# A two-layer encoder on one core: the mixers' tokens column by column, narrow windows for mixer B, and its probabilities turned by 12 short copies

## The chip, the cores and the metric

One core of one Trainium2 chip runs the whole program in one launch. The metric is the device time of a run in microseconds (us), lower is better. TensorE is called PE (its weight loads PEld), VectorE DVE, ScalarE ACT, GpSimd POOL; SP issues the transfers (DMA).

## The reference

256 tokens of width 2048 pass through two layers, all in fp32. Each layer has a mixer sub-layer and a feed-forward network; both are modulated by shifts, scales and gates that a vector `c` gives through a 2048 x 12288 matrix (adaLN).

```python
for l in range(DEPTH):
    mod = c_act @ ada_w[l] + ada_b[l]
    h = rmsnorm(x, norm_mix[l]) * (1.0 + sc_a) + sh_a
    qa, ka, va, qb, kb, vb, ga, gb = split_cols(h @ w_in[l])
    ya = window_attention(qa, ka, va, sink_a[l]) @ w_proj_a[l]
    yb = neighbourhood_attention(qb, kb, vb, rel_bias_b[l]) @ w_proj_b[l]
    merged = jax.nn.sigmoid(ga) * ya + jax.nn.sigmoid(gb) * yb
    x = x + gt_a * (merged @ w_out[l])
    h = rmsnorm(x, norm_ffn[l]) * (1.0 + sc_m) + sh_m
    g, v = jnp.split(depthwise_conv(h @ w_up[l], conv_w[l], conv_b[l]), 2, axis=-1)
    x = x + gt_m * ((jax.nn.silu(g) * v) @ w_down[l])
```

Mixer A (8 query heads, 2 key heads of 128) sees tokens at most 128 apart, with rotary positions and a sink. Mixer B (8 heads) sees the tokens as a grid of 4 rows by 64 columns; a token attends to all 4 rows and 16 neighbouring columns, with a learned bias by relative position. The feed-forward network is 5632 wide and has a convolution of width 3 over the tokens, in their plain order.

## The kernel before

**Data.** Features lie on the 128 partitions, 16 chunks of them, and the 256 tokens along the free axis. The weights come in one long stream `ws`, in the order in which they are used, as units of 16 blocks of 128 x 128 (1 MB). Each unit is loaded by SP into one of four raw buffers (line 315, a tile `w{layer}_{unit}`) and split in two halves `hl{layer}_{unit}_{half}` into a high and a low part: ACT copies (L326), DVE subtracts (L327). The high and low parts are rounded to fp32r, a format that PE takes faster than fp32. Each block then costs three matmuls of 256 columns (L343 to L345), or, where tokens and not features become the rows (the q, k, v columns), of 512 columns (L406 to L408). Between the units SP loads the adaLN matrix in blocks of 1 MB (`aw{layer}_{n}`, L232) into the same raw buffers; DVE multiplies and adds up each of them (L233) to 128 numbers. SP's transfers start in the order in which they are written, and they use eight completion semaphores in rotation.

**Start.** The first norm makes the chunks of h one by one (`normed`): ht (L497), its high part (ACT, L500) and its low part (L501). A chunk needs the adaLN numbers of its own blocks, so the start alternates aw blocks, units w_0, w_1, ... and the chunks of h. The columns of q, k, v are walked in two passes over k (`pi` 0 and 1) in nine groups of 512 columns (`g` 0 to 8). In layer 0 the tables of mask and of cosine and sine are loaded by `small` at the second pass's first group (L789).

**Attention.** Heads are Python generators that run beside the weight stream. `attend` (L646) does one head: scores `sc` for two halves of 128 queries (L651), in fp32 in layer 0 and as three fp32r matmuls in layer 1; one DVE instruction per half adds mask or bias and takes the maximum (L654), writing into the tile `p`; exp (L662) and scaling (L670) on ACT; then p is turned so that keys lie on partitions. In layer 0 PE turns it by four transposes (L681). In layer 1 DVE turns 32 x 32 blocks within each 32 partitions (L304) into free slots of the pack (the tile of q, k, v of four heads), and POOL moves the blocks between partitions by 16 copies of 32 x 128 back into p (L298). The result is split into `pT` (ACT L418, DVE L421), and six matmuls with v give `po` (L689). For mixer B, `head_b` (L876) loads the head's 256 KB bias by one transfer into one of two buffers `p` (L880), and the same tile then holds scores and probabilities until they are split.

**Merge.** The projections of the mixers are gated and added: `gated` (L434) makes m, L1014 adds ya, `split` (L423, L424) gives `merged`, the input of `w_out`. In layer 1 the gate of A is made by `bare_gate` from a tile z through tanh into `ya`.

**Order.** The program is written with generators; a scheduler then sets the order on each engine from estimated costs and priorities, so instructions move by more than the diff shows.

## Time and profile before

| | us |
|---|---|
| median of 3 runs | 2655.18 |
| lowest, highest | 2653.85, 2655.35 |
| the profiled execution | 2661.45 |
| its span in the trace | 2659.6 |

The profiled execution is 6.3 us longer than the median, and 1.85 us of it lie outside the span. Times inside the trace are counted from the span's start. The share of each engine and the groups of instructions are shown in the prediction; in the views quoted there "x16" is a count, "276/276/276" are the shortest, middle and longest duration in ns, and `[0.58 <-ACT h L500]` is idle time before an instruction and what ended it. Buffer numbers are left out of names there: `aw` is any block of the adaLN matrix, `hl` any half of a unit. Matmul durations overlap, so the distance between two starts is the cost, and not the duration. Stages used below, in us from the start: the start up to 100; mixer B's heads of layer 0 at 341 to 445; the merge of layer 0 about 490 to 595; mixer B's heads of layer 1 at 1622 to 1740.

### The profile page before, as it was taken

The numbers are of one execution on the slowest core, as the hardware profiler recorded it, in microseconds if no ns is written. First come the engines' busy times: TensorE is split into PE (matmuls) and PEld (weight loads), VectorE is DVE, ScalarE is ACT, GpSimd is POOL, SyncE is SP. The second block draws the span as 40 slices with busy tenths as digits, with TensorE's granted clock in tenths as the row PEclk, the third lists the DMA queues.
The fourth block names the chain that finished last, engine by engine and source line by source line (L and its number), as shares of the span: only waits on it lengthen the run. The fifth ranks groups of instructions, "written<-read, shape, count | busy, mean of one in ns | idle before, by whom it ended". The sixth has DMA issues, their size and how long they took to land.

```text
span 2659.6 us, 51014 instructions
## 1 busy us (share of the span) xinstructions
PE 2643.3 (99%) x21164; PEld 2557.9 (96%) x21164; DVE 2121.0 (80%) x2979; ACT 1408.9 (53%) x2280; POOL 228.2 (9%) x345
## 2 busy tenths in 40 slices
PE   9999999999999999999999999999999999999999
PEld 7888899999999999999998889999999999999999
DVE  8898998997987888788886778868888866655664
ACT  5445865456643555355554666654565445544553
POOL 0001100000000000000002558520000000000000
PEclk9999999999999999999999999999999999999999
DMA  9987779885777777877766666666747765555554
GB/s 371 349 329 292 267 294 356 316 339 184 295 272 289 284 287 285 306 296 285 283 221 253 249 234 232 253 258 257 283 178 287 297 252 191 192 196 194 196 191 143
DMA packets 102042, 700.42 MB, mean 263 GB/s; under 512 B 12721, under 2 KB 15025, under 8 KB 17969
## 3 DMA queue, kind: packets, MB, share of 16 engines
q1 hardware_dynamic: 101810, 697.17, 70.8%
q8 instruction: 165, 2.70, 0.4%
q14 instruction: 67, 0.55, 0.1%
HBM read 695.03 MB, written 2.10 MB: 262 GB/s over the span
## 4 chain that ended last, share of the span: by engine, by line
PE 86%; DMA 5%; DVE 5%; issue 2%; ACT 1%; POOL 0%; SPq 0%; DVEq 0%; ACTq 0%
PE ps L343 24%; PE ps L345 24%; PE ps L344 24%; DMA aw<-in_aw 4%; PE ps_t L408 4%; PE ps_t L407 4%; PE ps_t L406 4%; DVE hl L327 2%; DVE aw L233 1%; PE sc L651 1%; ACT hl L326 1%; PE po L689 1%; DMA w<-in_ws 1%; DVE u L1049 0%; POOL qrs L472 0%
## 5 line engine op out<-in xcount | busy, mean ns | idle before, releaser
L327 DVE TENSOR_TENSOR hl<-w,hl 128x1024 fp32r<-128x1024 f32 x928 | 1129.8, 1224 | 298.0 <-ACT hl L326 294.7
L326 ACT CAST hl<-w 128x1024 fp32r<-128x1024 f32 x928 | 969.8, 1049 | 719.7 <-PE ps L345 501.4
L343 PE MATMUL ps<-h,hl 128*128 128x256 f32 x3328 | 922.4, 277 | 1.3 <-DVE ya L970 0.6
L344 PE MATMUL ps<-h,hl 128*128 128x256 f32 x3328 | 919.6, 276 | 0.0
L345 PE MATMUL ps<-h,hl 128*128 128x256 f32 x3328 | 919.6, 277 | 0.0
L343 PEld LDWEIGHTS ps<-h,hl 128*128 128x128 f32 x3328 | 624.7, 188 | 2.4 <-DVE ya L970 0.8
L344 PEld LDWEIGHTS ps<-h,hl 128*128 128x128 f32 x3328 | 625.3, 188 | 0.4 <-DVE h L501 0.2
L345 PEld LDWEIGHTS ps<-h,hl 128*128 128x128 f32 x3328 | 624.4, 188 | 0.0
L233 DVE CUSTOM_DVE_ANT_0 aw<-aw,cact,ab 128x2048 f32<-128x2048 f32 x189 | 443.8, 2349 | 92.5 <-DMA aw<-in_aw 91.7
L406 PE MATMUL ps_t<-hl,h 128*128 128x512 f32 x576 | 223.0, 392 | 2.7 <-ACT h L500 2.0
L407 PE MATMUL ps_t<-hl,h 128*128 128x512 f32 x576 | 225.0, 391 | 0.3
L408 PE MATMUL ps_t<-hl,h 128*128 128x512 f32 x576 | 224.3, 390 | 0.0
L1049 DVE SCALAR_TENSOR_TENSOR u<-ps,cw,u 128x255 f32<-128x255 f32 x304 | 146.0, 480 | 62.0 <-ACT u L1047 58.1
L1047 ACT ACTIVATE u<-ps,cw 128x256 f32<-128x256 f32 x152 | 85.7, 564 | 155.4 <-PE ps L345 155.2
L343 PE MATMUL ps<-act_o,hl 128*128 128x256 f32 x512 | 142.0, 278 | 2.7 <-DVE u L1049 2.6
L345 PE MATMUL ps<-act_o,hl 128*128 128x256 f32 x512 | 142.1, 278 | 1.3 <-DVE hl L327 1.3
L344 PE MATMUL ps<-act_o,hl 128*128 128x256 f32 x512 | 142.0, 277 | 0.0
L345 PE MATMUL ps<-merged,hl 128*128 128x256 f32 x512 | 141.5, 277 | 0.0
L344 PE MATMUL ps<-merged,hl 128*128 128x256 f32 x512 | 141.5, 276 | 0.0
L343 PE MATMUL ps<-merged,hl 128*128 128x256 f32 x512 | 141.5, 277 | 0.0
L406 PEld LDWEIGHTS ps_t<-hl,h 128*128 128x128 f32 x576 | 107.9, 188 | 26.1 <-ACT h L500 3.0
L407 PEld LDWEIGHTS ps_t<-hl,h 128*128 128x128 f32 x576 | 108.1, 188 | 23.9 <-DVE hl L327 1.9
(244 smaller groups left out, 4800.3 us busy)
## 6 DMA issues: line engine op xcount, KB each, us to landing
w<-in_ws SPq DMA_DIRECT2D x463, 1024.0 KB, 4.9
aw<-in_aw SPq DMA_DIRECT2D x189, 1024.0 KB, 6.3
p<-in_bias SPq DMA_DIRECT2D x16, 256.0 KB, 4.5
x<-in_xT SPq DMA_DIRECT2D x4, 512.0 KB, 5.5
aw_o<-in_aw SPq DMA_DIRECT2D x2, 1024.0 KB, 12.4
out<-x SPq DMA_DIRECT2D x16, 128.0 KB, 3.2
w<-in_ws SPq DMA_DIRECT2D x2, 512.0 KB, 11.8
aw_b<-in_aw SPq DMA_DIRECT2D x1, 1024.0 KB, 18.1
```

The costliest lines, as they stand in the source:

```text
L233: nc.vector.tensor_tensor_reduce(out=raw[:], in0=raw[:], in1=cact[:], scale=1.0, scalar=ab[:, i : i + 1], op0=ALU.mult, op1=ALU.add, accum ...
L326: nc.scalar.copy(hl[:, 0], r)
L327: nc.vector.tensor_tensor(out=hl[:, 1], in0=r, in1=hl[:, 0].bitcast(F32), op=ALU.subtract)
L343: nc.tensor.matmul(out, hi, act[0], start=first, stop=False)
L344: nc.tensor.matmul(ps[:, :S], hi, act[1], start=False, stop=False)
L345: nc.tensor.matmul(out, lo, act[0], start=False, stop=last)
L406: nc.tensor.matmul(ps[:], xh, hi, start=kc == kcs[0], stop=False)
L407: nc.tensor.matmul(ps[:], xh, lo, start=False, stop=False)
L408: nc.tensor.matmul(ps[:], xl, hi, start=False, stop=kc == kcs[-1])
L651: nc.tensor.matmul(sc[:, t], q[i][:, t * P : (t + 1) * P], k[j], start=i + j == 0, stop=(i, j) == by(q)[-1])
L1047: nc.scalar.activation(out=u, in_=ps, func=AF.Identity, scale=w[:, 1:2], bias=w[:, 3:4])
L1049: nc.vector.scalar_tensor_tensor(out=u[:, to], in0=ps[:, of], scalar=w[:, j : j + 1], in1=u[:, to], op0=ALU.mult, op1=ALU.add)
```

## The change

**Token order.** Inside the mixers the tokens are put column by column: token (row r, column c) goes to place 4c + r instead of 64r + c. All that a token of one half of 128 may see in mixer B then lies within 160 neighbouring places (NEAR), keys 0 to 159 for the first half and 96 to 255 for the second. The order changes where h is made (`normed` writes ht with a step of four elements, 16 bytes, in the mixer's norm alone; in layer 1 `bare_gate` does the same for ya), and changes back at the merge: the add writes a new tile m2 with a step of 64 elements (256 bytes). The FFN sees the plain order.

**Tables and bias.** The rows of the bias, the mask, and the cosine and sine are loaded by `load_tokens`, four transfers of 64 partitions each instead of one; the bias's columns stay as they were and are read with a step by the reduce (L727 of the changed kernel), the mask's are put in order once by two POOL copies. `load_tables` moves the loading of mask, cosine and sine from the second pass's first group to behind the first pass's fourth group.

**Window.** Mixer B's scores, reduce, exp, scaling, and split work on 160 keys of 256 per half. The scores go into the head's own q and k slots of the pack and not into `p`, so the bias tile is free once the maximum is taken. In layer 0 POOL fills the remaining keys with zeros, and PE turns the tile as before. In layer 1 DVE turns the two windows in 32 x 32 blocks into a tile of their own, `turned`, and POOL moves the blocks by 12 copies (ten of 32 x 64, two of 32 x 32). pT of mixer B is one tile in each layer, cleared once outside the windows; `po` stays six matmuls of 256 columns. Squares' two small buffers become one tile with two halves, which shares its place with `turned`.

```diff
 BLOCK = 32
+GRID_H = S // GRID_W
+NEAR = P + BLOCK
...
 QK_STEPS = 3
-MOVED = [(0,0), (8,8)]
+MOVED = [0, 8]
+WINDOWS_FROM = [8, 0]
 STEPS = [1, 1]
...
+    def by_rows(t):
+        return t.rearrange("p (r c) -> p r c", c=GRID_W)
+    def rows_by_column(t):
+        return t.rearrange("p (r c) -> p c r", c=GRID_W)
+    def by_columns(t):
+        return t.rearrange("p (c r) -> p c r", r=GRID_H)
+    def columns_by_row(t):
+        return t.rearrange("p (c r) -> p r c", r=GRID_H)
+    def sheared(t, at, step, n):
+        (part, tile_step, (s, _)) = t.ap
+        return bass.AP(t.tensor, t.offset + at * s, [part, (tile_step[0] + step * s, 2), (s, n)])
+    def near(t):
+        return sheared(t, 0, S - NEAR, NEAR)
+    def load_tokens(dst, src):
+        rows = src.rearrange("(q w c) h f -> w q c h f", q=GRID_H // 2, w=2)
+        for w in range(2):
+            for q in range(GRID_H // 2):
+                nc.sync.dma_start(dst[q::2, w], rows[w, q])
     def place(tag, n, dt, name):
...
+    def turned_near(p):
+        turned = ev.tile([P, 2, S], F32, name="turned", tag="r", bufs=1)[:]
+        nc.vector.transpose(out=near(turned), in_=near(p))
+        for a in range(P // BLOCK):
+            for d in (-1, 0, 1):
+                b = (a + d) % 4
+                dst, src = p[b * BLOCK : (b + 1) * BLOCK], turned[a * BLOCK : (a + 1) * BLOCK]
+                if a + d == b:
+                    to, of = (sheared(x, i * BLOCK, P, BLOCK) for x, i in ((dst, a), (src, b)))
+                else:
+                    t = int(d < 0)
+                    to, of = (x[:, i, P - BLOCK * i : P + BLOCK * (1 - i)] for x, i in ((dst, 1 - t), (src, t)))
+                nc.gpsimd.tensor_copy(out=to, in_=of)
     def unit_steps(l, u, by_halves=False):
...
+    def split_near(dst, src, held):
+        high, low = near(dst[:, 0]), near(dst[:, 1])
+        copied = nc.scalar.copy(high, near(src))
+        if held:
+            tc.keep_in_program_order(copied)
+        nc.vector.tensor_tensor(out=low, in0=near(src), in1=high.bitcast(F32), op=ALU.subtract)
     def half_tanh(dst, src, **kw):
...
             self.acc = ev.tile([P, S], F32, name="sqa", tag="sqa", bufs=1)
+            self.pair = ev.tile([P, 2, S], F32, name="sqs", tag="r", bufs=1)
             self.ps = ax.tile([P, 2, 2], F32, name=name, tag="ss", bufs=1)
         def add(self, mo):
-            sq = self.acc if mo == 0 else ev.tile([P, S], F32, name="sq", tag="r", bufs=2)
-            nc.scalar.activation(out=sq[:], in_=x[:, mo], func=AF.Square)
+            sq = self.acc[:] if mo == 0 else self.pair[:, mo % 2]
+            nc.scalar.activation(out=sq, in_=x[:, mo], func=AF.Square)
             if 0 < mo < KC - 1:
-                nc.vector.tensor_tensor(out=self.acc[:], in0=self.acc[:], in1=sq[:], op=ALU.add)
+                nc.vector.tensor_tensor(out=self.acc[:], in0=self.acc[:], in1=sq, op=ALU.add)
             if mo == KC - 1:
...
             sh = mod[:, 3 * w * KC + kc : 3 * w * KC + kc + 1]
+            to, of, roots = (t[:], x[:, kc], rbs[:]) if w else (columns_by_row(t[:]), by_rows(x[:, kc]), by_rows(rbs[:]))
             nc.vector.scalar_tensor_tensor(
-                out=t[:], in0=x[:, kc], scalar=amod[:, w, kc : kc + 1], in1=rbs[:], op0=ALU.mult, op1=ALU.mult
+                out=to, in0=of, scalar=amod[:, w, kc : kc + 1], in1=roots, op0=ALU.mult, op1=ALU.mult
             )
...
-    def attend(q, k, v, p, mask, scale, sink, o, rows=None):
+    def attend(q, k, v, p, mask, scale, sink, o, rows=None, turned_in=None):
+        window = sink is None
+        n = NEAR if window else S
+        def part(t):
+            return slice(t * (S - n), t * (S - n) + n)
             for i, j in by(q):
-                nc.tensor.matmul(sc[:, t], q[i][:, t * P : (t + 1) * P], k[j], start=i + j == 0, stop=(i, j) == by(q)[-1])
+                nc.tensor.matmul(
+                    sc[:, t, :n], q[i][:, t * P : (t + 1) * P], k[j][:, part(t)], start=i + j == 0, stop=(i, j) == by(q)[-1]
+                )
         m = sm.tile([P, 2], F32, name="m", tag="m")
         for t in range(2):
+            to, of, add = p[:, t, part(t)], sc[:, t, :n], mask[:, t]
+            if window:
+                first = part(t).start // GRID_H
+                to, of = by_columns(to), by_columns(of)
+                add = rows_by_column(add)[:, first : first + n // GRID_H]
             nc.vector.tensor_tensor_reduce(
-                out=p[:, t], in0=sc[:, t], in1=mask[:, t], scale=scale, scalar=-3.0e38 if sink is None else sink,
+                out=to, in0=of, in1=add, scale=scale, scalar=-3.0e38 if sink is None else sink,
                 op0=ALU.add, op1=ALU.max, accum_out=m[:, t : t + 1],
         for t in range(2):
-            nc.scalar.activation(out=p[:, t], in_=p[:, t], func=AF.Exp, bias=nm[:, t : t + 1], accum_out=den[:, t : t + 1])
+            e = p[:, t, part(t)]
+            nc.scalar.activation(out=e, in_=e, func=AF.Exp, bias=nm[:, t : t + 1], accum_out=den[:, t : t + 1])
         if sink is not None:
...
         for t in range(2):
-            nc.scalar.activation(out=p[:, t], in_=p[:, t], func=AF.Copy, scale=ri[:, t : t + 1])
+            e = p[:, t, part(t)]
+            nc.scalar.activation(out=e, in_=e, func=AF.Copy, scale=ri[:, t : t + 1])
+        if window and rows is None:
+            nc.gpsimd.memset(sheared(p, NEAR, -NEAR, S - NEAR), 0.0)
         yield
         if rows is not None:
-            turned_blocks(p[:], rows(), 2)
-            for _ in range(STEPS[sink is None]):
+            if window:
+                turned_near(p)
+            else:
+                turned_blocks(p, rows(), 2)
+            for _ in range(STEPS[window]):
                 yield
...
                     nc.tensor.transpose(tp[:, k, t * P : (t + 1) * P], p[:, t, k * P : (k + 1) * P], ident[:])
-        pT = at.tile([P, 2, 2, S], F32R, name="pT", tag="pT", bufs=1)
-        split(pT, tp[:], held=rows is not None)
+        pT = turned_in() if window else at.tile([P, 2, 2, S], F32R, name="pT", tag="pT", bufs=1)
+        if window:
+            split_near(pT, tp, rows is not None)
+        else:
+            split(pT, tp[:], held=rows is not None)
         v = v()
...
+    def load_tables():
+        seen = at.tile([P, 2, S], F32, name="seen", tag="p")
+        load_tokens(seen[:], a["maskA"])
+        mask = const.tile([P, 2, S], F32, name="maskA")
+        for t in range(2):
+            nc.gpsimd.tensor_copy(out=by_columns(mask[:, t]), in_=rows_by_column(seen[:, t]))
+        cs = const.tile([P, 2, 2, HALF], F32, name="cs")
+        for f in range(2):
+            load_tokens(cs[:, f], a["cs"][:, f])
+        tables.extend((mask, cs))
     def small(l):
-        if l == 0:
-            tables.extend((load(a["maskA"], [P, 2, S], "maskA"), load(a["cs"], [P, 2, 2, HALF], "cs")))
         cs = tables[1]
...
                     z, sh = bare.level(ps, 0.5)
-                    half_tanh(ya[:, mo], z[:], bias=sh[:, :1])
+                    half_tanh(columns_by_row(ya[:, mo]), by_rows(z[:]), bias=sh[:, :1])
...
             yield from attend(
-                q, k, v, p, tables[0], SCALE, sink[:, i : i + 1], lambda: oA[i], rows if i < MOVED[l][0] else None
+                q, k, v, p[:], tables[0], SCALE, sink[:, i : i + 1], lambda: oA[i], rows if i < MOVED[l] else None
             )
             p = at.tile([P, 2, S], F32, name="p", tag="p")
-            nc.sync.dma_start(p[:], a["bias"][l, hb])
+            load_tokens(p[:], a["bias"][l, hb])
             q = in_halves(b[:, 8 + i], f"qB{l}_{hb}", "qh", l in SCORES_3)
             yield from attend(
-                q, k, lambda: in_halves(v[:, :, i * HEAD : (i + 1) * HEAD], f"vB{l}_{hb}", "vh", True), p, p, 1.0, None,
-                lambda: oB_of(hb), (lambda: b[:, i : 9 + i : 8]) if hb < MOVED[l][1] else None,
+                q, k, lambda: in_halves(v[:, :, i * HEAD : (i + 1) * HEAD], f"vB{l}_{hb}", "vh", True),
+                b[:, i : 9 + i : 8], p[:], 1.0, None, lambda: oB_of(hb), True if hb >= WINDOWS_FROM[l] else None,
+                turned_in,
             )
+        windows = []
+        def turned_in():
+            if not windows:
+                windows.append(at.tile([P, 2, 2, S], F32R, name=f"pTB{l}", tag="pT", bufs=1))
+                for i in range(2):
+                    nc.gpsimd.memset(sheared(windows[0][:, i], NEAR, -NEAR, S - NEAR).bitcast(F32), 0.0)
+            return windows[0]
...
                 pss = st.tokens(h, part)
+                if l == 0 and pi == 0 and g == 3:
+                    load_tables()
                 if pi == max(0, len(parts) - 2) and g == 0:
...
                 gated(z[:], gb[mo], ps)
-                nc.vector.tensor_tensor(out=z[:], in0=z[:], in1=ya[:, mo], op=ALU.add)
-                split(merged[mo], z[:], 0.5)
+                both = ev.tile([P, S], F32, name="m2", tag="z")
+                nc.vector.tensor_tensor(
+                    out=rows_by_column(both[:]), in0=by_columns(z[:]), in1=by_columns(ya[:, mo]), op=ALU.add
+                )
+                split(merged[mo], both[:], 0.5)
```

At the start, SP's queue before, from the seventh block aw of layer 0 on (`seen` is the mask as loaded, `cs` cosine and sine; the last number of a name is a counter):

```order
L232 DMA aw0_6_332<-in_aw 128x2048
L315 DMA w0_3_335<-in_ws 128x2048
L232 DMA aw0_7_371<-in_aw 128x2048
L315 DMA w0_4_383<-in_ws 128x2048
L232 DMA aw0_8_415<-in_aw 128x2048
L315 DMA w0_5_422<-in_ws 128x2048
```

And of the changed kernel:

```order
L267 DMA aw0_6_332<-in_aw 128x2048
L365 DMA w0_3_335<-in_ws 128x2048
L223 DMA seen_349<-in_maskA 64x256 x4
L223 DMA cs_357<-in_cs 64x1x16 x8
L267 DMA aw0_7_388<-in_aw 128x2048
L365 DMA w0_4_400<-in_ws 128x2048
L267 DMA aw0_8_432<-in_aw 128x2048
L365 DMA w0_5_439<-in_ws 128x2048
```

Twelve small transfers stand between w0_3 and aw0_7 that stood further down before; the rest keeps its order.

In layer 0's mixer B, DVE before, from the first half of unit 54 on (packB0_0 is the pack of heads 0 to 3, sc scores, m the maximum, tp the turned probabilities; ISA rows are the reduces):

```order
L327 TENSOR_TENSOR hl0_54_0_3517<-w0_54_3515,hl0_54_0_3517 128x1024
L233 ISA aw0_45_3636,mod0_172<-aw0_45_3636,cact_100,ab0_173 128x2048
...
L421 TENSOR_TENSOR pT_3207<-tp_3202,pT_3207 128x512
L654 ISA p_3191,m_3216<-sc_3213,p_3191 128x256
...
L659 TENSOR_SCALAR nm_3219<-m_3216 128x2
...
L327 TENSOR_TENSOR hl0_54_1_3520<-w0_54_3515,hl0_54_1_3520 128x1024
...
L327 TENSOR_TENSOR hl0_55_0_3580<-w0_55_3578,hl0_55_0_3580 128x1024
L327 TENSOR_TENSOR hl0_55_1_3583<-w0_55_3578,hl0_55_1_3583 128x1024
```

And of the changed kernel:

```order
L377 TENSOR_TENSOR hl0_54_0_3549<-w0_54_3547,hl0_54_0_3549 128x1024
L727 ISA packB0_0_224,m_3238<-sc_3235,p_3208 128x160
...
L484 TENSOR_TENSOR pTB0_3227<-tp_3222,pTB0_3227 128x2x160
L732 TENSOR_SCALAR nm_3241<-m_3238 128x2
L377 TENSOR_TENSOR hl0_54_1_3552<-w0_54_3547,hl0_54_1_3552 128x1024
...
L377 TENSOR_TENSOR hl0_55_0_3612<-w0_55_3610,hl0_55_0_3612 128x1024
...
L377 TENSOR_TENSOR hl0_55_1_3615<-w0_55_3610,hl0_55_1_3615 128x1024
...
L268 ISA aw0_45_3668,mod0_172<-aw0_45_3668,cact_100,ab0_173 128x2048
```

The reduction of aw0_45 moves from ahead of the head's reduces to behind both halves of unit 55, and the halves of unit 54 come closer together. On SP, aw0_45 follows the bias of head 2 and w0_56 that of head 3; before, aw0_45 and w0_56 stood ahead of head 2's.

## The prediction

> **What bounds the kernel now.** I read the page first, its busy times and the chain that ended last.
>
> ```profile
> span 2659.6 us, 51014 instructions
> PE 2643.3 (99%) x21164; PEld 2557.9 (96%) x21164; DVE 2121.0 (80%) x2979; ACT 1408.9 (53%) x2280; POOL 228.2 (9%) x345
> PE 86%; DMA 5%; DVE 5%; issue 2%; ACT 1%; POOL 0%; SPq 0%; DVEq 0%; ACTq 0%
> ```
>
> TensorE is busy for 2643.3 of 2659.6 us. So an edit can save time only where it takes columns from TensorE, or where TensorE waits; and it costs time only where it makes TensorE wait. Next come the windows of the stages that the change touches (columns: stretch, its length, busy time and count of PE, PEld, DVE, ACT, POOL, the granted clock, the DMA share, GB/s).
>
> ```profile
> 25.00:50.00 25.00, 23.22 (x96) 17.70 (x97) 22.64 (x26) 16.47 (x24) 0.00 (x0) 1.00 0.96 385
> 50.00:75.00 25.00, 24.44 (x143) 21.07 (x142) 22.29 (x23) 12.29 (x20) 0.00 (x0) 1.00 0.96 355
> 75.00:100.00 25.00, 24.72 (x211) 24.31 (x211) 20.49 (x24) 14.82 (x25) 0.00 (x0) 1.00 0.94 361
> 350.00:400.00 50.00, 50.00 (x410) 48.62 (x410) 47.96 (x87) 30.02 (x58) 0.00 (x0) 1.00 0.84 315
> 400.00:450.00 50.00, 50.00 (x435) 49.79 (x434) 45.18 (x62) 27.94 (x50) 0.00 (x0) 1.00 0.96 360
> 495.00:545.00 50.00, 50.00 (x440) 50.00 (x439) 48.80 (x86) 25.95 (x44) 0.00 (x0) 1.00 0.83 307
> 1650.00:1700.00 50.00, 50.00 (x439) 50.00 (x438) 42.06 (x74) 30.60 (x58) 31.51 (x61) 1.00 0.64 240
> ```
>
> Three kinds of place: the start (25 to 100), where PE is not full and the transfers are at 94 to 96%; layer 0's mixer B and merge (350 to 595), where PE is full but VectorE has only 1.2 to 4.8 us idle in 50; and layer 1's mixer B (1650 to 1700), where PE is full and VectorE, ScalarE and GpSimd have 8 to 19 us to spare. A matmul's duration here overlaps the next one's, so the count says more than the busy time: 410 matmuls in 350 to 400 against 440 elsewhere is the price of the fp32 scores and transposes.
>
> **Term a, the start.** The tables of mask, cosine and sine now go on SP behind unit w_3 as 4 + 8 small transfers, ahead of aw_7 (the seventh adaLN block behind the first). In the trace of before SP issued and VectorE and PE took:
>
> ```profile
> 33.78 0.33 SPq L232 DMA_DIRECT2D aw<-in_aw  x1
> 38.37 0.33 SPq L315 DMA_DIRECT2D w<-in_ws  x1
> 40.64 0.33 SPq L232 DMA_DIRECT2D aw<-in_aw  x1
> ...
> w<-in_ws SPq DMA_DIRECT2D x1, 1024.0 KB, 9.0
> aw<-in_aw SPq DMA_DIRECT2D x1, 1024.0 KB, 6.9
> w<-in_ws SPq DMA_DIRECT2D x1, 1024.0 KB, 4.9
> ...
> 96.52 0.43 SPq L178 DMA_DIRECT2D maskA<-in_maskA  x1
> 96.99 0.43 SPq L178 DMA_DIRECT2D cs<-in_cs  x1
> ...
> maskA<-in_maskA SPq DMA_DIRECT2D x1, 256.0 KB, 6.1
> ...
> 40.53 2.36 DVE L327 TENSOR_TENSOR hl<-w,hl 128x1024 fp32r<-128x1024 f32 x2
> 42.80 2.34 DVE L233 CUSTOM_DVE_ANT_0 aw<-aw,cact,ab 128x2048 f32<-128x2048 f32 x1
> 45.38 0.48 DVE L497 SCALAR_TENSOR_TENSOR ht<-x,amod,rbs 128x256 f32<-128x256 f32 x1
> 46.44 0.48 DVE L501 SCALAR_TENSOR_TENSOR h<-ht,mod,h 128x256 fp32r<-128x256 f32 x1 [0.58 <-ACT h L500]
> ...
> 45.88 0.39 PE L408 MATMUL ps_t<-hl,h 128*128 128x512 f32 x1
> 46.46 0.50 PE L406 MATMUL ps_t<-hl,h 128*128 128x512 f32 x1 [0.20 <-ACT h L500]
> ```
>
> The three landing times are those of the issues at 29.24 (w_3), 33.78 (aw_7) and 38.37 (w_4), each read in a stretch around its issue. So w_3 lands at 38.2 and aw_7 at 33.78 + 6.9 = 40.7. VectorE reduces aw_7 at 42.80, then the next chunk of h is made from it, and PE waits for that chunk at 46.46: here VectorE is on the path without a gap, with about 2.1 us of lead on the transfer. After the change the program's rotation of eight completion semaphores lets the fourth cosine transfer (the eighth behind w_3) start only when w_3 has landed, 38.2. Five cosine transfers then follow at 0.47 us each (96.52 to 96.99), so aw_7 issues at 38.2 + 5 x 0.47 = 40.5, 6.8 us later than now. With the 4.9 us of the nearest transfer issued at such a time it lands at 45.4, and VectorE wants it at 42.80: 2.6 us late. PE already waits 0.2 us there, in the last row; I take **+2.4**. The bounds: 0 if VectorE finds half a unit to split in the gap and PE's later waits (0.56 and 0.28 us in the next two windows, and VectorE's 2.7 and 4.5 us idle there) swallow it; +4 if aw_7 lands with 6.9 us as it did, 47.4, less some of that idle time. Behind aw_7 stand w_4 and aw_8 on SP; they were issued at 38.37 and 40.64 and come 2 us late too, in the same shift, not a second one. The tables' removal from 96.5 is **0** (to -0.3): PE lost only 0.28 us in that whole window.
>
> **Terms c and g, narrower scores.** PE issues as many matmuls as before; only the score matmuls of mixer B shrink, from 256 to 160 columns.
>
> ```profile
> L651 PE MATMUL sc<-packB x32: 379/379/382, 341.6 to 426.7; 128*128 128x256 f32 x32
> L651 PE MATMUL sc<-kB,qB x48: 276/276/276, 1622.8 to 1731.6; 128*128 128x256 f32 x48
> ...
> 341.63 0.60 PE L651 MATMUL sc<-packB 128*128 128x256 f32 x2
> 342.06 0.49 PE L681 MATMUL tp<-ident,p 128*128 128x128 f32 x3
> ...
> 1622.80 0.84 PE L651 MATMUL sc<-kB,qB 128*128 128x256 f32 x6
> 1623.48 0.28 PE L343 MATMUL ps<-h,hl 128*128 128x256 f32 x1
> ...
> 623.05 0.60 PE L461 MATMUL ssm<-mean,sqa 128*128 128x1 f32 x4
> 623.52 0.36 PE L345 MATMUL ps<-bare_a,hl 128*128 128x258 f32 x1
> ```
>
> Layer 0 works in fp32. Two 256-column matmuls stand 342.06 - 341.63 = 0.43 us, 0.216 each; the 128-column transposes (0.49 - 0.27) / 2 = 0.108: 0.844 ns per column at both widths. At 160 columns that is 0.135, so 32 x (0.216 - 0.135) = **-2.6 us**, in a stretch where PE is full. Bounds 0 (if the stage is already held by VectorE) and -2.6.
>
> Layer 1 works in fp32r. Six matmuls of 256 columns take 1623.48 - 1622.80 = 0.68, 0.113 each, 0.44 ns per column. Purely by width 160 columns would take 0.071, 48 x 0.042 = -2.0. But matmuls of one column, with 128x128 weights as well, still stood (623.52 - 623.05) / 4 = 0.117 apart: a floor that columns don't set. I take **-0.5**, a quarter of the way to the bound -2.0, since that floor is the nearest narrow row. No fp32r matmul in the trace has fewer than 256 columns, so the other bound is that narrow ones go at the fp32 rate, 0.27 us each: 48 x (0.27 - 0.117) = +7.3 (rival 2).
>
> The Trainium skill (TensorE: Matmul & The Clock Gate, section "Wait — 56ns, not 53.3ns?") puts warm matmuls at columns over 2.4 GHz plus some 2.5 ns, which for 160 columns is an estimate of 0.069 us and -2.1 us for the 48; the rows at 256 columns (0.113 measured, 0.109 by the rule) agree roughly, the one-column rows (0.117) do not, and I go by the latter.
>
> **Terms b, d and f, VectorE's new shapes.** These are the strided stores (16-byte steps in ht, 256-byte steps in the merge's m2), strided reads of the bias, and the narrower softmax.
>
> ```profile
> L1014 DVE TENSOR_TENSOR m<-m,ya 128x256 f32<-128x256 f32 x16 | 6.7, 420 | 0.1
> L654 DVE CUSTOM_DVE_ANT_0 p<-sc,p 128x256 f32<-128x256 f32 x16 | 6.2, 418 | 0.2 <-PE sc L651 0.2
> L421 DVE TENSOR_TENSOR pT<-tp,pT 128x512 fp32r<-128x512 f32 x8 | 5.5, 684 | 0.5 <-ACT pT L418 0.5
> L327 DVE TENSOR_TENSOR hl<-w,hl 128x1024 fp32r<-128x1024 f32 x16 | 19.5, 1219 | 0.3 <-ACT hl L326 0.3
> ```
>
> (The first and last are of 490 to 535, the middle two of 341 to 445; busy, mean ns.) From 256 to 512 elements costs 684 - 418 = 0.27 us, so 1.04 ns per element and 0.15 fixed. *Softmax, layer 0*: a reduce of 160 elements costs 0.32 (16 x 0.10 less), a split of 320 0.48 (8 x 0.20 less): 3.2 us less VectorE work where PE is full. Cover: PE's own work; it only lengthens the splits' lead. **0**, to -1.0 for the short waits left there. The zero fills go to GpSimd, idle in layer 0 (0.00 in both windows); in layer 1 it drops from 31.5 of 50 us. *Bias in four transfers*: 32 issues more or less 0.47 us on SP, 15 us over 100; aw_45 now stands behind head B2's bias and w_56 behind B3's, and each of these waits for the reduce of the head two before. VectorE also takes aw_45 later, behind two halves of w_55, so its buffer and its need move together: **0**. If w_56 came late, its cover is the four raw buffers, some 20 us of PE work.
>
> *Strides*: no row has a strided fp32 store. Lower bound 0 (an element a cycle, whatever the address); upper, twice the 0.97 ns per element of the L327 row's 1024, +0.25 us per 256 elements. ht: about 6 of its 16 in stretches of the start where VectorE is the path, 0 to +1.4 (term b). Merge: 16 x 0.25 = 4.0 against 0.5 us idle in 45, with the hi/lo halves 2.7 us or more ahead of PE: 0 to +3 (term f). I take **0** for both, since VectorE's cost in all rows goes by elements.
>
> **The sum** against the profiled execution: +2.4 (a) - 2.6 (c) - 0.5 (g), the rest at 0, = **-0.7 us**: a span of 2658.9 for 2659.6, a run of 2660.75 for 2661.45. That execution stood 6.3 us above the median of the runs, 2655.18; against that median the forecast is **2654.5 us**. About 0.2% (5.3 us) is what a measurement of this kernel can tell from no change.
>
> **Rivals.** *1, strided stores cost two cycles.* Then b and f come at their ends: +2.4 - 2.6 - 0.5 + 1.4 + 3.0 = +3.7, **2658.9**. For it: VectorE at 48.80 of 50 in the merge. Against: 2.7 us lead of the halves. Chance 0.20. It decides from about 0.15 us per store on, where 16 of them eat idle time and lead. The Trainium skill (Advanced Engine Details and Errata, section "SBUF Cachelines") has 16-byte lines and wants at least two hits on each; both new stores step a line or more per element, so by that rule this rival would hold. No row here shows it.
>
> *2, slower: narrow fp32r matmuls at the fp32 rate.* The place is layer 1's 48 scores, at 0.27 us each: +7.3 on the forecast's other terms without g's -0.5, **2662.3**. For it: PE has no slack there (50.00 of 50), and every fp32r matmul of the kernel so far has 256 columns or more. Against: the one-column rows show no such penalty, though they are fp32. It decides from 0.22 us a matmul on. Chance 0.17.
>
> *3, faster: the start swallows the tables.* VectorE splits a half in the gap (a = 0), and c, d, g and the tables' absence come at their ends, -2.6 - 1.0 - 2.0 - 0.3 = -5.9, **2649.3**. For it: 2.7 and 4.5 us VectorE idle in the next windows. Against: PE waits at 46.46 for this very chunk. Chance 0.16.
>
> *4, slower: SP's queue in layer 0's mixer B.* If a bias waits for its tile with w_56 behind it, one unit comes late by up to the 2 x 1.22 us of its splits and again at the next bias: about 3 x 2.4 = 7 us on the forecast, **2661.7**. The 410 matmuls and 0.96 DMA share of the two windows speak for it, the four raw buffers against. Chance 0.07.
>
> **How the numbers follow.** Forecast 0.40 (its own range 2651 to 2658.5), rivals 0.20, 0.17, 0.16, 0.07. Slower by over 0.2% (above 2660.5): nearly all of 2 (0.15), some of 1 (0.09), most of 4 (0.05), a little of the forecast: 0.31. Faster (below 2649.9): most of 3 (0.12) and a little more: 0.14. Rest 0.55. The range takes in the centres of all rivals: 2648.5 to 2663.5.
>
> **What would show it.** a: aw_7 issued near 40.5 and VectorE idle for 2 us or more ahead of its reduce near 43; if there is no such gap, a falls. c: score matmuls of layer 0 0.135 apart. g: those of layer 1 0.09 to 0.117 apart (rival 2: 0.27). b and f: ht near 477 ns and the merge's add near 420 (rival 1: 700 or so). d: PE full in 350 to 450 with more than 410 and 435 matmuls. What would prove the whole wrong is a PE wait of several us in a stage that the change doesn't touch, by an order that I read as neutral.

## The result, and the profile after

| | median, us | runs | ratio to before, 95% interval |
|---|---|---|---|
| before | 2655.20 | 2653.43 to 2662.75, 13 runs | |
| changed | 2663.54 | 2658.50 to 2667.17, 13 runs | 1.0027 [1.0018, 1.0036] |
| changed, second set of runs | 2661.41 | 2659.44 to 2663.11, 11 runs | 1.0023 [1.0015, 1.0032] |

The change makes the kernel slower by 6.5 to 8.3 us, 0.25 to 0.31% of the medians beside it. The first profile of the changed kernel is of its shortest run, 2658.5 us, and the profile of before was of one of its longer ones, 2661.45; so the two spans, 2656.7 and 2659.6, stand the wrong way round. In before's profile PE waits 2.6 us near 782 and then runs its matmuls some 4% slower for about 90 us, 6.0 us in all, which is most of what it lies above its median; of the other profiles only that of e15_pool_act_plan shows the like. Stages have to be compared one by one, and the spread has to be explained too.

One measure serves for that besides the views. Every trace of this study holds 21164 matmuls, so the n-th of one trace can be set beside the n-th of another. The difference of their two starts says how far one run is behind the other at that point, and what it grows by from the first matmul of a stage to the last is what the stage cost. Below, "2 us late from 340 to 480" means that: the difference to before's trace grew by 2 us between the matmuls that start at 340 and 480 us in before's trace; "made up" means that it shrank.

The changed kernel's page, busy times and the chain that ended last:

```profile
span 2656.7 us, 51093 instructions
PE 2639.9 (99%) x21164; PEld 2554.6 (96%) x21164; DVE 2120.9 (80%) x2979; ACT 1400.8 (53%) x2280; POOL 209.5 (8%) x327
PE 87%; DVE 6%; DMA 3%; issue 2%; ACT 2%; POOL 0%; SPq 0%; DVEq 0%; ACTq 0%
```

TensorE and VectorE are as busy as before, and still TensorE is the bound. The windows of the stages (columns as in the prediction) tell more:

```profile
25.00:50.00 25.00, 20.73 (x87) 15.39 (x85) 21.54 (x25) 12.27 (x18) 4.09 (x2) 1.00 0.80 313
...
35.00:40.00 5.00, 4.21 (x18) 2.79 (x17) 3.98 (x5) 3.22 (x5) 1.44 (x2) 1.00 0.39 135
40.00:45.00 5.00, 4.95 (x22) 3.77 (x21) 4.87 (x4) 3.32 (x5) 2.65 (x1) 1.00 0.57 167
...
50.00:75.00 25.00, 23.79 (x122) 19.62 (x122) 21.72 (x24) 13.87 (x20) 0.00 (x0) 1.00 0.99 369
350.00:400.00 50.00, 49.92 (x421) 48.96 (x421) 44.94 (x86) 29.22 (x63) 1.69 (x7) 1.00 0.82 303
400.00:450.00 50.00, 49.78 (x433) 49.58 (x432) 44.50 (x64) 25.52 (x50) 0.52 (x2) 1.00 0.89 339
495.00:545.00 50.00, 49.35 (x432) 49.15 (x431) 49.59 (x79) 25.04 (x45) 0.00 (x0) 1.00 0.79 290
```

The start lost 2.5 us of busy TensorE in its first window, and the DMA share fell from 0.96 to 0.80: at 35 to 45 us the DMA engines were idle for half of the time (0.39 and 0.57). Mixer B of layer 0 does 421 matmuls in 350 to 400 instead of 410, the gain; from 340 to 480 the kernel makes up 1.6 us. The merge lost eight matmuls (432 for 440), with VectorE at 49.59 of 50, and is 0.9 us late. The start, on SP, VectorE and PE, in the changed kernel:

```profile
30.58 2.46 SPq L223 DMA_DIRECT2D seen<-in_maskA  x4
33.09 8.02 SPq L223 DMA_DIRECT2D cs<-in_cs  x8
41.21 0.53 SPq L267 DMA_DIRECT2D aw<-in_aw  x1
...
42.08 2.80 DVE L377 TENSOR_TENSOR hl<-w,hl 128x1024 fp32r<-128x1024 f32 x2
47.02 2.35 DVE L268 CUSTOM_DVE_ANT_0 aw<-aw,cact,ab 128x2048 f32<-128x2048 f32 x1 [2.15 <-DMA aw<-in_aw]
49.61 0.67 DVE L557 SCALAR_TENSOR_TENSOR ht<-x,amod,rbs 128x256 f32<-128x256 f32 x1
...
47.34 0.39 PE L458 MATMUL ps_t<-hl,h 128*128 128x512 f32 x1
50.88 0.50 PE L456 MATMUL ps_t<-hl,h 128*128 128x512 f32 x1 [3.15 <-ACT h L560]
```

Eight cosine transfers hold SP for 8 us, aw_7 issues at 41.21 (33.78 before), VectorE stands idle for 2.15 us before it, and PE waits 3.15 us for the chunk of h behind it. VectorE's two halves at 42.08 took 2.80 instead of 2.36 us, beside GpSimd's two copies of the mask (4.09 us busy, none before); but they ended 2.15 us before the block was there, so this did not make its reduce later. ht takes 0.67 us instead of 0.48.

VectorE's new shapes over the whole program, and the score matmuls (the first two rows are groups: busy, mean ns; the next two starts and spans on PE):

```profile
L1120 DVE TENSOR_TENSOR m<-m,ya 128x256 f32<-128x256 f32 x32 | 20.2, 633 | 0.2
L727 DVE CUSTOM_DVE_ANT_1 packB<-sc,p 128x160 f32<-128x160 f32 x32 | 13.0, 439 | 0.6 <-PE sc L717 0.5
...
346.77 0.44 PE L717 MATMUL sc<-packB 128*128 128x160 f32 x2
347.04 0.27 PE L761 MATMUL tp<-ident,p 128*128 128x128 f32 x1
...
1619.97 0.80 PE L717 MATMUL sc<-kB,qB 128*128 128x160 f32 x6
1620.60 0.32 PE L393 MATMUL ps<-h,hl 128*128 128x256 f32 x1
1620.75 0.28 PE L394 MATMUL ps<-h,hl 128*128 128x256 f32 x1
1620.87 0.28 PE L395 MATMUL ps<-h,hl 128*128 128x256 f32 x1
```

The merge's add takes 0.63 us (0.42 before). The reduce over 160 keys takes 0.44, more than the 0.42 that 256 keys took. The strided read of the bias is the new step in it, and a likely reason, but no run measures it apart. Layer 0's scores stand (347.04 - 346.77) / 2 = 0.135 us apart, layer 1's (1620.60 - 1619.97) / 6 = 0.105. That is a mean of two sizes: in each of the eight groups of six the first matmul is followed after 0.07 us, and the other five after 0.11, as with 256 columns. The first matmul behind the group then takes 1620.75 - 1620.60 = 0.15, where the next takes 0.12.

### The profile page after: what moved, and what is told of

It is laid out like the page before. It is cut to its first block, busy times and chain, and to the rows that moved or that the text cites. A ratio compares the mean times of both kernels' runs of the same rounds, so it can differ in the third digit from the quotient of the medians.

```text
span 2656.7 us, 51093 instructions
## 1 busy us (share of the span) xinstructions
PE 2639.9 (99%) x21164; PEld 2554.6 (96%) x21164; DVE 2120.9 (80%) x2979; ACT 1400.8 (53%) x2280; POOL 209.5 (8%) x327
## 4 chain that ended last, share of the span: by engine, by line
PE 87%; DVE 6%; DMA 3%; issue 2%; ACT 2%; POOL 0%; SPq 0%; DVEq 0%; ACTq 0%
PE ps L393 25%; PE ps L395 24%; PE ps L394 24%; PE ps_t L458 4%; PE ps_t L457 4%; PE ps_t L456 4%; DVE hl L377 2%; DMA aw<-in_aw 2%; DVE aw L268 1%; ACT hl L376 1%; DMA w<-in_ws 1%; PE sc L717 1%; PE po L772 1%; POOL qrs L531 0%; PE warm L499 0%
```

## The experiments

All differences are to before's median in the same batch (2654.0 for e1 to e4, 2654.3 for e5 to e8, 2654.9 for e9 to e12, 2654.5 for e13 to e16).

### e1 to e4: where the tables stand, and the strided stores

e1_tables_late, of the changed kernel:

```diff
-                if l == 0 and pi == 0 and g == 3:
-                    load_tables()
...
     def small(l):
+        if l == 0:
+            load_tables()
```

> The changed kernel with the tables' loading back at its old place (second pass, first group). Theory A (the twelve small transfers behind w_3 hold up aw_7): VectorE's 2.15 us idle before aw_7's reduce and its two stretched instructions (+0.8 us, GpSimd's mask copies beside them) go, so 3.0 us less than the changed kernel's 2663.5, about 2660.5. Theory B (the strided stores set the loss): no change, 2663. Theory C (the late tables only shift which transfers are late, and later waits give the gain back or add to it): 2663 or more, with PE waits past 96 us that the changed kernel does not have.

Measured: 2665.21 us in 5 runs, +11.2 on before (1.0041 [1.0028, 1.0054]). Theory A's place fell, its mechanism did not. SP and PE there:

```profile
100.08 6.12 SPq L223 DMA_DIRECT2D cs<-in_cs  x8
106.25 0.59 SPq L181 DMA_DIRECT2D gains<-in_gains  x1
...
108.68 1.24 SPq L267 DMA_DIRECT2D aw<-in_aw  x1
...
121.19 0.73 PE L456 MATMUL ps_t<-hl,h 128*128 128x512 f32 x2 [3.44 <-ACT hl L376]
```

The eight small transfers now block SP at 100 us; the adaLN block behind the tables issues at 108.68 (100.74 in the kernel before), and PE waits 3.44 us at 121. The cost goes with the twelve transfers, not with the place; at 50 us the wait is gone, as theory C had it.

e2_early_tables, of the kernel before (mask and cosine in plain rows):

```diff
+        mask = const.tile([P, 2, S], F32, name="maskA")
+        load_rows(mask[:], a["maskA"])
+        cs = const.tile([P, 2, 2, HALF], F32, name="cs")
+        for f in range(2):
+            load_rows(cs[:, f], a["cs"][:, f])
...
+                if l == 0 and pi == 0 and g == 3:
+                    load_tables()
```

> The kernel before with nothing but the tables moved: mask, cosine and sine as twelve transfers of the same sizes (4 of 64 KB, 8 of 4 KB), in plain row order, behind w_3. Theory A: VectorE idle some 2 us before aw_7's reduce, 2655.2 + 2.4 = 2657.6, and no more spread than before. Theory C: 2660 or more, spread over 5 us and more as the changed kernel is. If the start absorbs it: 2655.

Measured: 2659.38, +5.4 (1.0017 [1.0009, 1.0026]), 2657.99 to 2660.10 in 11 runs. Twice what was expected, with a narrow spread: the tables alone are the largest part of the loss, but not of its spread. SP, VectorE and PE there:

```profile
32.46 9.85 SPq L790 DMA_DIRECT2D cs<-in_cs  x8
42.41 0.53 SPq L232 DMA_DIRECT2D aw<-in_aw  x1
...
47.34 2.35 DVE L233 CUSTOM_DVE_ANT_0 aw<-aw,cact,ab 128x2048 f32<-128x2048 f32 x1 [4.13 <-DMA aw<-in_aw]
...
51.01 0.80 PE L406 MATMUL ps_t<-hl,h 128*128 128x512 f32 x1 [4.41 <-ACT h L500]
```

aw_7 issues at 42.41, VectorE stands idle for 4.13 us before it, and PE waits 4.4 us at 51. From 45 to 75 us this run is 5.3 us late, about the whole of its +5.4.

e3_plain_stores, of the changed kernel:

```diff
-            to, of, roots = (t[:], x[:, kc], rbs[:]) if w else (columns_by_row(t[:]), by_rows(x[:, kc]), by_rows(rbs[:]))
+            to, of, roots = (t[:], x[:, kc], rbs[:])
...
-                    out=rows_by_column(both[:]), in0=by_columns(z[:]), in1=by_columns(ya[:, mo]), op=ALU.add
+                    out=both[:], in0=z[:], in1=ya[:, mo], op=ALU.add
```

> The changed kernel with contiguous stores in the three places of the reordering (ht of the mixer's norm, ya of the bare gate, the merge's m2): the tokens stay in row order there, so the reordering is left out; the instructions are the same in number and shape. Theory B: ht falls from 0.67 to 0.48 us and the merge's add from 0.63 to 0.42; the 0.6 us of the start's path and the 0.8 us stall of the merge near 543 go: 1.4 to 1.7 us less, about 2662. Theory A alone: 2663.5. If strided stores are behind the spread as well: 2658 and runs within 3 us of each other.

Measured: 2658.76, +4.7 (1.0016 [1.0007, 1.0025]); 2655.87 to 2662.24. Against before that is 1.8 to 3.6 us less than the changed kernel's +6.5 and +8.3, more than the 1.4 to 1.7 that the waits of its first profile held; ht is back at 0.48 us, the merge's add at 0.43. The spread stays near 6 us.

e4_late_and_plain has both edits.

> Both edits together: tables at their old place and contiguous stores (the reordering is left out as before). What is left of the change are the narrow windows, the four-part bias transfers and the 12 copies. Theories A and B together, if the terms add: 2663.5 - 3.0 - 1.5 = 2659; against before, whose undisturbed runs are near 2653.5 to 2655, the windows' -1.8 should then leave 2652 to 2653. The gap between these two numbers, 2659 and 2652, is the part of the loss that no profile has shown yet; where the run falls tells how large it is.

Measured: 2659.93, +5.9 (1.0021 [1.0012, 1.0030]). With the tables late but still on SP, PE waits 3.3 us near 122, and the run is 6.5 us late from 110 to 130, so this run could not remove term a; it confirms e1.

### e5 to e8: the queue, the bias, the merge

e5_tables_pool, of the changed kernel:

```diff
-                nc.sync.dma_start(dst[q::2, w], rows[w, q])
+                eng.dma_start(dst[q::2, w], rows[w, q])
...
-        load_tokens(seen[:], a["maskA"])
+        load_tokens(seen[:], a["maskA"], nc.gpsimd)
...
-            load_tokens(cs[:, f], a["cs"][:, f])
+            load_tokens(cs[:, f], a["cs"][:, f], nc.gpsimd)
```

> The changed kernel with the same twelve table transfers issued by GpSimd, whose queue has semaphores of its own; the scheduler puts them at the very start there. Theory D (they cost because they stand in SP's queue: the rotation of eight semaphores makes the fourth cosine transfer wait for w_3, and aw_7 waits behind): aw_7 issues near 34 as in the kernel before, PE's 3 to 4.6 us wait at 52 and its like at 124 are gone, 2663.5 - 4.5 = 2659. Theory E (the small transfers themselves hold up the DMA engines, on whatever queue): 2663, with aw_7 landing 2 us late or more though issued in time.

Measured: 2660.04, +5.8 (1.0020 [1.0011, 1.0029]). SP's and PE's rows at the place of the wait:

```profile
34.90 0.33 SPq L267 DMA_DIRECT2D aw<-in_aw  x1
...
47.96 0.50 PE L456 MATMUL ps_t<-hl,h 128*128 128x512 f32 x1 [0.35 <-ACT h L560]
```

aw_7 issues at 34.90 and PE's wait is 0.35 us instead of 3.15, as theory D had it. The edit changed two things, though: the transfers left SP's queue, and they moved to 1.3 to 13.0 us, so this run alone does not tell the queue from the moment. Against theory E speaks the changed kernel's DMA share at 35 to 45 us, 0.39 and 0.57: half of the time the DMA engines had nothing to do. Only 0.7 to 2.5 us came back at the end (+5.8 against +6.5 and +8.3): in this profile mixer B of layer 0 is 0.7 us late and the merge 4.4, where VectorE waits for adaLN blocks (5.2 us between 480 and 640) and PE for VectorE near 600.

e6_bias_one, of the changed kernel:

```diff
-            load_tokens(p[:], a["bias"][l, hb])
+            nc.sync.dma_start(p[:], a["bias"][l, hb])
```

> The changed kernel with each head's bias loaded by one transfer of 256 KB in plain row order instead of four of 64 partitions; the rows of the bias are then in the wrong order, which this run leaves out. Theory G (the 64 transfers in the place of 16 hold up SP and w units in mixer B, rival 4 of the prediction): 3 us or more less than the changed kernel, 2660, and less spread. If they are hidden: 2663.5 within 1.5.

Measured: 2661.51, +7.2 (1.0024 [1.0014, 1.0035]): 2.0 us below one median of the changed kernel and level with the other. In the medians the bias in four transfers costs nothing that can be told from noise, and the 3 us or more of theory G are not there. The traces show a small cost all the same. From 340 to 480 us the three kernels with windows and one transfer per bias (e6, e13 and e14) make up 2.0 to 2.1 us on before, and the nine with four transfers 1.6 at best; two of the nine are even late, by 0.7 (e5) and 0.4 us (e15), and there PE waits 1.5 and 1.3 us for a head's scaled probabilities, which it does in none of the three.

e7_pool_and_plan, of e5_tables_pool:

```diff
-ADA_PLAN_0 = [(38, 32), (58, 48), (76, 66), (84, 70), (98, 80), (108, 80), (231, 143)]
+ADA_PLAN_0 = [(38, 32), (58, 48), (76, 66), (80, 68), (92, 70), (100, 76), (108, 80), (231, 143)]
```

> The kernel of e5_tables_pool with another plan of the adaLN blocks in layer 0: fewer of their reduces (2.35 us of VectorE each) during the merge, two or three instead of five or six, the rest later where VectorE has 13 us idle in 50. Theory B' (the merge's strided adds cost 0.21 us each on a VectorE that is full there, 49.97 of 50 busy, and PE waits 1 to 3.5 us for halves at 543 to 604): 2 us less than e5_tables_pool, 2657, and less spread. If the merge's adds don't matter: equal to e5_tables_pool.

Measured: 2658.20, +3.9 (1.0015 [1.0006, 1.0024]), 1.8 less than e5, though the runs of the two overlap (2656.81 to 2660.30 and 2657.37 to 2663.94). Its trace points to VectorE's load in the merge as the cause: from 480 to 610 us it is not late at all, where e5 is 4.4 us. But the wait moved on, 1.4 us on PE between 600 and 640, and from 610 to 640 it is 2.1 us late.

e8_strided_merge, of the kernel before:

```diff
-                nc.vector.tensor_tensor(out=z[:], in0=z[:], in1=ya[:, mo], op=ALU.add)
-                split(merged[mo], z[:], 0.5)
+                both = ev.tile([P, S], F32, name="m2", tag="z")
+                nc.vector.tensor_tensor(
+                    out=both[:].rearrange("p (r c) -> p c r", c=GRID_W), in0=z[:].rearrange("p (c r) -> p c r", r=4),
+                    in1=ya[:, mo].rearrange("p (c r) -> p c r", r=4), op=ALU.add,
+                )
+                split(merged[mo], both[:], 0.5)
```

> The kernel before with only the merge's add changed: it writes a new tile m2 with the 256-byte step, as the changed kernel does (the tokens then come out in a wrong order; the amounts of work are the same). Theory B': 16 x 0.21 = 3.4 us more VectorE work in layer 0's merge, PE waits of 0.8 us near 543 and up to 1.5 near 600, 2654 + 1 to 3.5 = 2655 to 2657.5, with more spread than before (which is 4 us). If VectorE's lead hides it: 2654.

Measured: 2655.80, +1.5 (1.0005 [0.9996, 1.0014], so the interval still holds no change). Its group of the adds between 485 and 545, and PE's only wait between 480 and 640:

```profile
L1015 DVE TENSOR_TENSOR m<-m,ya 128x256 f32<-128x256 f32 x16 | 10.1, 629 | 0.1
...
PE ps L343 <- DVE m L434: 0.6, 1, 0.6
```

From 480 to 610 us this run is 2.1 us late; the rest of 16 x 0.21 = 3.4 us lies within VectorE's lead. Its runs lie within 2.1 us of each other, so more spread, which was expected, did not come.

### e9 to e12: the spread, and whether the costs add

e9_changed_again is the changed kernel.

> The changed kernel once more, for a second profile: the first is of its shortest run, 2658.5, five below its median. Theory H (the merge's fuller VectorE frees the raw buffers late, so adaLN blocks land late in 540 to 620 by a length that differs from run to run): 2663.5 again, and a profile nearer to the median shows VectorE waiting 4 us or more for aw between 480 and 640 (1.8 in the first profile, 1.5 in the kernel before) and PE more than 1 us of waits there. If the difference lies elsewhere, in the start or in layer 1, the same window shows 2 us or less.

Measured: 2661.41, +6.5, and a profile of span 2661.2. The signs of theory H are there (VectorE waits 4.9 us for adaLN blocks, PE 2.8 us), at a median 2 us below the one expected. They do not prove its reason: in e13_windows_alone, without any strided store, VectorE waits 5.3 us for such blocks in the same window, and PE not at all. The windows show two more things. First the start: PE's wait, then windows of 1 us (the granted clock is the third number from the end):

```profile
50.24 0.50 PE L456 MATMUL ps_t<-hl,h 128*128 128x512 f32 x1 [3.17 <-ACT h L560]
...
50.00:51.00 1.00, 0.76 (x3) 0.54 (x4) 0.48 (x1) 1.00 (x2) 0.00 (x0) 1.00 1.01 426
51.00:52.00 1.00, 1.00 (x5) 0.62 (x4) 0.84 (x1) 1.00 (x3) 0.00 (x0) 0.90 1.00 426
52.00:53.00 1.00, 0.96 (x2) 0.50 (x2) 1.00 (x2) 1.00 (x3) 0.00 (x0) 0.50 1.07 451
53.00:54.00 1.00, 1.00 (x4) 0.77 (x3) 1.00 (x2) 0.12 (x2) 0.00 (x0) 0.50 0.97 401
54.00:55.00 1.00, 1.00 (x4) 0.81 (x3) 1.00 (x1) 1.00 (x2) 0.00 (x0) 0.50 1.00 418
55.00:56.00 1.00, 1.00 (x5) 0.77 (x5) 1.00 (x3) 0.92 (x1) 0.00 (x0) 0.89 1.00 303
```

The wait is as long as in the first profile (3.17 and 3.15 us), but here TensorE's clock is halved afterwards, from about 51.8 to 55.2: 3.4 us at half speed. The first profile shows a granted clock of 1.00 throughout 50 to 58. From 45 to 75 us it is 3.3 us late and this one 4.0, so the half clock cost about 0.7 us here, where PE is not full. Second, the residual stage behind the merge, VectorE, PE's waits from 480 to 640, and windows:

```profile
593.65 2.35 DVE L268 CUSTOM_DVE_ANT_0 aw<-aw,cact,ab 128x2048 f32<-128x2048 f32 x1 [2.45 <-DMA aw<-in_aw]
...
PE ps L395 <- DVE hl L377: 2.1, 1, 2.1
PE ps L393 <- DVE m L492: 0.7, 1, 0.7
...
595.00:600.00 5.00, 2.89 (x17) 2.70 (x16) 5.00 (x9) 0.43 (x2) 0.00 (x0) 0.79 0.54 208
600.00:601.00 1.00, 1.00 (x7) 1.00 (x6) 1.00 (x3) 1.00 (x2) 0.00 (x0) 0.50 0.96 352
601.00:602.00 1.00, 1.00 (x9) 1.00 (x8) 1.00 (x2) 0.32 (x1) 0.00 (x0) 0.83 1.02 369
```

VectorE stands 2.45 us before a late adaLN block with a half of a unit queued behind it; PE waits 2.1 us for that half and then runs at half clock again. The first profile has neither. The two profiles are of the same program, so their matmuls can be compared one by one: of the 4.5 us between them 4.1 arise between 585 and 615 us, at this second place, and 0.7 in the start. Whether the longest runs, up to 2667.17, hold more of the same, no profile shows.

e10_act_reorders, of e5_tables_pool:

```diff
-                nc.vector.tensor_tensor(
-                    out=rows_by_column(both[:]), in0=by_columns(z[:]), in1=by_columns(ya[:, mo]), op=ALU.add
-                )
+                nc.vector.tensor_tensor(out=z[:], in0=z[:], in1=ya[:, mo], op=ALU.add)
+                nc.scalar.copy(rows_by_column(both[:]), by_columns(z[:]))
```

> The kernel of e5_tables_pool with the merge's add contiguous and the change back of the token order made by one more ACT copy per chunk (m2 from m, strided). ACT has half its time free in the merge. Theory B' (VectorE's 0.21 us per strided add is the cost): the waits of 540 to 605 go, 2660.0 - 2 to 3 = 2657 to 2658. If any longer chain from gated to merged costs as much: 2660.

Measured: 2659.79, +4.9 (1.0019 [1.0011, 1.0028]), against e5's +5.8. The late waits near 600 are gone from its profile, but PE now waits 1.6 us at the merge's first matmuls, for `gated`: so the longer chain may cost nearly what it saves; the 0.9 us between the two medians are not clear of noise.

e11_strided_ht, of the kernel before:

```diff
+            to, of, roots = (t[:], x[:, kc], rbs[:]) if w else (t[:].rearrange("p (c r) -> p r c", r=4), x[:, kc].rearrange("p (r c) -> p r c", c=GRID_W), rbs[:].rearrange("p (r c) -> p r c", c=GRID_W))
...
-                out=t[:], in0=x[:, kc], scalar=amod[:, w, kc : kc + 1], in1=rbs[:], op0=ALU.mult, op1=ALU.mult
+                out=to, in0=of, scalar=amod[:, w, kc : kc + 1], in1=roots, op0=ALU.mult, op1=ALU.mult
```

> The kernel before with nothing but ht of the mixer's norm stored in the 16-byte step (the merge doesn't change the order back, so tokens come out in a wrong order). ht 0.48 to 0.67 us: in the start some four of them stand on VectorE's path by 100 us: +0.8, 2655. If the stride also delays what stands behind it there: 2656 or more.

Measured: 2655.65, +0.8 (1.0006 [0.9997, 1.0015]): the 0.8 expected, though not clear of no change.

e12_costs_alone joins the edits of e2, e8 and e11.

> The kernel before with all three suspected costs and none of the narrow windows: early tables in twelve transfers, strided ht, strided merge add (mask in plain order, so the output differs). If the terms simply add: 2654.1 + 5.2 (e2_early_tables) + 1.5 (e8_strided_merge) + 0.8 = 2661.6. If they feed one another in the merge: 2663 to 2665, the changed kernel's 2663.5 plus the windows' 1.2 to 1.8. Below 2660 a cost is left that none of the three holds.

Measured: 2661.47, +6.6 (1.0022 [1.0012, 1.0032]), 1.1 us below the sum of the three parts, 5.4 + 1.5 + 0.8 = 7.7, and within what these runs can tell: among themselves the three costs add. It is as slow as the changed kernel, although it lacks the narrow windows and so should be 1.2 to 1.8 us behind.

### e13 to e16: where the windows' saving went

e13_windows_alone, of the changed kernel, has the edits of e3 and e6 and the plain tables:

```diff
+        mask, cs = load(a["maskA"], [P, 2, S], "maskA"), load(a["cs"], [P, 2, 2, HALF], "cs")
...
+        if l == 0:
+            load_tables()
```

> The changed kernel without its costs: tables in two plain transfers at their old place, contiguous stores in all three places, each bias by one transfer. The reordering of tokens, mask and bias rows is left out; the narrow windows, pT of its own, the zero fills and the 12 copies stay. Theory W1 (the windows' 1.2 to 1.8 us of TensorE reach the end): 2654.5 - 1.5 = 2653. Theory W2 (VectorE and the adaLN transfers set the end of the merge and of the residual stage, so what TensorE saves in mixer B it waits for by 620 us): 2654.5, and in the profile TensorE is 1.2 us or more ahead of the kernel before at 415 us and level with it at 620.

Measured: 2652.59, -1.9 (0.9992 [0.9984, 1.0001]), and the view of PE's waits lists none between 480 and 640. The interval still holds no change, but the trace is clear: from 340 to 480 us the kernel makes up 2.1 us on before, and it keeps them to 640. So W1 holds where the costs are absent, and W2 falls.

e14_windows_plan is e13_windows_alone with the plan of e7_pool_and_plan.

> The same with the plan of e7_pool_and_plan (three or four adaLN reduces fewer in the merge, later instead). W2: VectorE has 7 us more in the merge, the windows' gain survives: 2653. W1: as e13_windows_alone. If the later reduces only move the wait to 620 us, as in e7_pool_and_plan (1.57 us there): 2655.

Measured: 2654.72, +0.2 (1.0000 [0.9991, 1.0009]), 2.1 worse than e13. The plan costs by itself, which e16_before_plan, the kernel before with that plan, confirms:

> The kernel before with the other plan of adaLN blocks alone. If the plan as such costs or saves anything, it shows here: 2654.5 if it is neutral; 2656 if the wait near 620 of e7_pool_and_plan is the plan's own.

Measured: 2658.03, +3.5 (1.0011 [1.0003, 1.0020]); PE waits 2.5 us in one piece between 480 and 640. So the gain of e7 over e5 is net of a loss that the plan brings. With the same plan on both sides the windows are worth 3.3 us (2654.72 in e14 against 2658.03), a second sign that their saving reaches the end.

e15_pool_act_plan joins the edits of e7_pool_and_plan and e10_act_reorders.

> The changed kernel with its costs mended where they can be: tables on GpSimd's queue, the change back of the order on ACT, and the other plan. If the three mends add: 2658.2 (e7_pool_and_plan) less the 0.5 to 1.5 us that e10_act_reorders still lost near 542, about 2657; no better than the kernel before (2654.5) in any theory.

Measured: 2661.80, +7.3 (1.0030 [1.0020, 1.0040]). The three mends do not add; no version that keeps the order of the tokens right was faster than the kernel before.

## Why the prediction was wrong, step by step

**Term a, the start: mechanism right, size wrong.** aw_7 was to issue at 40.5 and did at 41.21 (e2: 42.41); VectorE was to idle 2 us or more and did 2.15 (e2: 4.13). The fourth cosine transfer waited for w_3 as worked out: it starts at 37.99, and w_3 lands at 37.98. But +2.4 became +5.4 (e2), for two reasons. The first is when the block lands: 45.4 by the prediction, 47.0 in the changed kernel and 47.3 in e2. The five cosine transfers from that one on took 3.1 to 3.2 us and not 5 x 0.47 = 2.35, and then either aw_7 took 5.8 us instead of 4.9 (changed kernel) or w_3 landed 1.1 us later than in before's trace (e2). So PE waited 3.2 to 4.4 us. The second is that a wait of more than 2 us was followed by a half clock of TensorE in ten of twelve cases (last section), which the prediction, pricing a wait at its own length, did not have. Its upper bound of +4 had room for the late landing, but not for the half clock.

**Terms b and f, the strides: taken at 0, and that was the wrong end.** The stores cost 0.19 us (ht) and 0.21 us (merge), close to the upper end of 0.25, so rival 1's mechanism was the true one. b is +0.8 (e11, forecast 0 to 1.4); f alone +1.5 (e8, forecast 0 to 3). Neither median is clear of no change by itself, but f shows in the traces: 2.1 us late in the merge in e8, 2.0 in e12. "VectorE's cost in all rows goes by elements" held for contiguous rows, and there were no others to read. (The 0.97 ns per element beside it is not what its row gives: 1219 ns for 1024 elements are 1.19 each, or 1.04 beyond the fixed 0.15 us. The upper end becomes 0.27 us by that, and nothing else changes.) The rule of the Trainium skill that stood beside rival 1 (Advanced Engine Details and Errata, section "SBUF Cachelines") agrees: both stores, one line or more per element, cost some 0.8 ns per element more (0.20 us in 256).

**Term c: the spacing right, the sum a little too large.** A score matmul of layer 0 stands 0.135 us before the next, as worked out. But in both kernels 8 of the 32 are followed by another kind of matmul after only 0.03 us, whatever their width, so the 32 went from 5.6 to 3.6 us: -2.0 and not -2.6. The stage agrees: 2.1 us made up in e13 and e14. With g the windows bring -1.9 at the end (e13; forecast -3.1, within the interval, which reaches from -4.2 to +0.3).

**Term g: about nothing.** The mean spacing is 0.105 against 0.113 us, 48 x 0.008 = -0.4 (forecast -0.5). The floor that the prediction took from the one-column rows is there for five matmuls of six; the sixth shrank by its whole width, to 0.07, so that the mean came near is partly luck. And the gain did not last: from 1600 to 1740 us every kernel with windows is 0.1 us late against before. Part of it goes to the matmul behind each group, whose successor starts later. Rival 2 falls: narrow fp32r matmuls are not slower.

**Term d: no run prices it.** The reduce got no shorter (0.44 for 0.42 us), so half of the 3.2 us less VectorE work never came; nothing contradicts the 0. Rival 4 falls at its price of 7 us; by the traces the bias in four transfers costs 0.4 to 2.9 us in mixer B (see e6), and whether that comes about in rival 4's way is not shown. Rival 3 falls: the start did not swallow the tables.

**The sum: the parts were taken one by one, and they meet in the merge.** What each stage cost, in us late (minus: made up), is this:

| profile of | start, 45 to 75 | layer 0's mixer B, 340 to 480 | merge, 480 to 610 |
|---|---|---|---|
| changed, first | 3.3 | -1.6 | 0.9 |
| changed, second (e9) | 4.0 | -0.9 | 5.2 |
| e5_tables_pool | 0.5 | 0.7 | 4.4 |
| e6_bias_one | 4.6 | -2.0 | 5.1 |
| e2_early_tables, no windows | 5.3 | 0.1 | 0.9 |
| e8_strided_merge, no windows | 0.0 | -0.3 | 2.1 |
| e12_costs_alone, no windows | 5.0 | 0.2 | 2.0 |
| e13_windows_alone | -0.1 | -2.1 | 0.0 |

The three columns of a row add up to within 1.6 us of how much longer that execution took than before's median. The first step that fails is the price of the start's wait (a: +2.4 where e2 measured +5.4), the second the choice of 0 for f. The third is the adding up. Strides without windows cost 2.0 to 2.1 us in the merge, and windows without strides nothing (e13, e4) or 1.1 (e3). Strides and windows together cost 0.9 in the changed kernel's first profile, but 3.7 to 5.2 in the four others with the same plan of adaLN blocks, that of e1 among them; with fewer of the blocks' reduces in the merge (e7) they cost nothing there. A likely reason is that the windows let TensorE reach the merge earlier while VectorE is slowed there, so the lead is used up from both ends; that is argued from the profiles, and no run separated it from the moment at which the adaLN block lands. The medians alone would not show it: the parts give 5.4 + 1.5 + 0.8 - 1.9 = +5.8, the changed kernel +6.5 and +8.3, and each part is uncertain by 2 us or so.

The range 2648.5 to 2663.5 ended 0.04 us below the median of the 13 runs, and the second set's median, 2661.41, lies inside it. That is chance; the forecast of 2654.5 and its terms a, f and the adding up were off in both.
